# Output projection with seven products: weight sums in half steps, fetches moved, output stage ordered from a list of durations

## The chip, the cores and the metric

The kernel runs on one core of a Trainium2 chip. The metric is the device time of one execution in microseconds (us); lower is better. Five engines take part, each with its own queue of instructions that it works off in order: TensorE (PE, with its weight loads shown apart as PEld), VectorE (DVE), ScalarE (ACT), GpSimd (POOL) and SyncE (SP). SP only starts DMA transfers here; POOL and ScalarE start some too. L12 stands for line 12 of the kernel before.

## The reference

One layer of a hybrid trunk: 1024 latent tokens and 128 context tokens of width 1024 go through a modulated norm, one input projection, a gMLP group and an attention group of 4 heads, and one output projection. The change lies in the softmax loop and in the output projection:

```python
def _back(x, gate, a_out, attn, g_b, w_o):
    y = jnp.concatenate([a_out, attn * jax.nn.silu(g_b)], axis=-1) @ w_o
    return x + gate * y
...
        s = jnp.concatenate(logits, axis=-1).astype(jnp.float32) * ATTN_SCALE
        p = jax.nn.softmax(s, axis=-1).astype(v_all.dtype)
        return jnp.einsum('bhqk,bkhv->bqhv', p, v_all)
...
    y_prompt = _rmsnorm(xp, final_g)
    y_sample = _rmsnorm(xs, final_g)
```

All of it is fp32, and w_o is 1024 x 1024.

## The kernel before

**Tiles.** The tokens are nine tiles of 128: tiles 0 to 7 hold the latent tokens, tile 8 the context. An fp32 matmul is done as three passes of a faster type: each operand is split into a part hi and a remainder lo, and hi x hi, lo x hi and hi x lo are added in PSUM. The split is a cast (ScalarE or POOL, `pool_copy` L115) and a subtraction on VectorE (`lo_of` L112), called the low below.

**Softmax loop** (about 320 to 525 us). Each round takes two heads: their scores on TensorE, maxima on VectorE, exponentials on ScalarE (L1490), and `divide` (L1493 to 1501), which normalises a head's row e on POOL (L1496). Merged with the scores of a round runs the value stream of the round before: transposes of e (pT, L1554), their split (ph L1558 on ScalarE, pl L112 on VectorE), three matmuls each, and the result joined into mixB (L1599).

**Weight sums.** The output projection multiplies pairs of tiles by w_o with seven half-size products instead of eight. They need four sums T1 to T4 of the blocks of w_o (each 512 x 512, in four pieces). A unit `t_unit` (L1860) makes a quarter of one k piece of all four: `t_load` (L1854) brings traw from memory, four subtractions on POOL (L809), two casts on ScalarE (thi, L1876), two lows on VectorE, eight stores to the DRAM buffer tdram (SP). There are eight units; `divide` starts one behind each of the heads 5 to 12. `t_fetch` and `t_piece` (L1891, L1896) bring pieces back through POOL's queue.

**Loads of w_o.** The blocks themselves come through `wo_piece` and `next_load` (L1634 to 1662): SP loads piece k into wor, POOL casts two halves into area, VectorE makes their lows. Pieces 0 to 4 share one raw buffer; a load starts only when the low before it has been read. Pieces 5 to 7 use the slots of e.

**Output stage.** `pair(n)`, n = 0 to 3, takes two tiles and runs its products in the order EARLY, the last pair in FINAL (L1791, L1792). The left operand of a product is a block of the two tiles (A11, A12, A22) or a sum of blocks (S1 to S4, made by four `s_sums` on POOL); it is split into one of the five slots of `ring` (L1812) by `split` (L2067: two copies on ScalarE, one of them to PSUM, and a low on VectorE). A product is 12 matmuls, four k pieces of three passes, into one PSUM bank. What comes after a product (`after`, L2111) adds it to others on VectorE, multiplies by the gate and adds the residual row xr on POOL or VectorE; `norm` and `finish_last` give the final norm and the stores of y. The context tile needs all eight pieces of w_o and is multiplied by `plain` without sums, between the last transposes.

**What sets the order.** Nothing is scheduled at run time: Python code places each instruction. `run` carries a model clock forward and `later(dt, fn)` puts work at a modelled time; `merged` mixes two lists by their modelled lengths. At each softmax round a line asks whether a pool is to be opened. A class `Plan` is there too, used in an earlier stage: it holds steps with an engine, a cost, the steps they depend on, a priority and resources, and places at each modelled moment the step of best priority that can run.

## Time and profile before

| what | us |
|---|---|
| median of 3 runs | 643.28 |
| the runs | 643.28, 644.11, 641.68 |
| the profiled execution | 645.44 |
| its span, first to last instruction | 643.7 |
| PE busy | 605.0 |
| PEld busy (overlaps PE) | 543.6 |
| DVE busy | 435.8 |
| ACT busy | 328.6 |
| POOL busy | 215.4 |

The mean granted TensorE clock of the profiled execution is 0.974. The span is cut into 40 equal slices, each with a digit for the busy tenths of an engine; a row of the timeline gives the start in us, the duration, the engine, the line, the operation and its operands, and in brackets how long the engine was idle just before and which instruction ended that. The rows of transfers at the end of a page give the destination, the source, the queue, the number of transfers, the size of one and the median time from issue to landing.

### The profile page before, as it was taken

To read this page: it belongs to the slowest core of one execution; us is meant where nothing else is said; L and a number is where in the kernel's file an instruction comes from. 1 tells how busy PE (TensorE), PEld (TensorE's weight loads), DVE (VectorE), ACT (ScalarE), POOL (GpSimd) and SP (SyncE) were. 2 spreads that over 40 slices of the span, in tenths; PEclk is the share of its full clock that TensorE was granted. 3 is DMA by queue.
4 is the path that set the end of the run, shared out by engine and by line. 5 is a ranking of instruction groups with operands and counts; after the bars stand their busy time and mean duration, and the time that the engine had idled before them with its cause. 6 is when DMAs were issued, how large, how long until landed. Compare 5 with 4: busy or idle time off the path is not lost. (4 is left out here: it accounts for less than half of the span.)

```text
span 643.7 us, 10209 instructions
## 1 busy us (share of the span) xinstructions
PE 605.0 (94%) x3659; PEld 543.6 (84%) x3659; DVE 435.8 (68%) x931; ACT 328.6 (51%) x758; POOL 215.4 (33%) x262
## 2 busy tenths in 40 slices
PE   8899999999999999999999978899999999799980
PEld 6678899999989999999988867799999988587760
DVE  4793468996655685666787756577767755387885
ACT  6566753345333345555665555555466433365541
POOL 2470111000000002333634755235322346267652
PEclk9999999999999999999999988899999999899995
DMA  8982010003332141000021656400111129933311
GB/s 320 403 329 66 1 34 10 24 1 130 131 133 66 44 162 38 13 1 1 8 66 50 196 168 203 137 1 2 34 34 34 56 78 369 348 112 118 130 67 66
DMA packets 31779, 67.33 MB, mean 105 GB/s; under 512 B 3424, under 2 KB 18672, under 8 KB 31216
## 3 DMA queue, kind: packets, MB, share of 16 engines
q1 hardware_dynamic: 28704, 58.09, 26.0%
q0 software_dynamic: 2880, 8.39, 3.7%
q8 instruction: 29, 0.48, 0.3%
q14 instruction: 22, 0.18, 0.1%
q10 hardware_dynamic: 144, 0.20, 0.1%
HBM read 53.45 MB, written 13.21 MB: 104 GB/s over the span
## 5 line engine op out<-in xcount | busy, mean ns | idle before, releaser
L1496 POOL TENSOR_SCALAR e<-e,rs 128x1280 f32<-128x1280 f32 x32 | 45.1, 1409 | 108.7 <-DVE rs L1495 88.2
L112 DVE TENSOR_TENSOR pl<-pT,ph 128x512 fp32r<-128x512 f32 x81 | 55.2, 685 | 34.0 <-ACT ph L1558 32.9
L1490 ACT ACTIVATE e<-s,nb,scl 128x256 f32<-128x256 f32 x64 | 56.0, 879 | 28.9 <-DVE nb L1484 28.9
L1558 ACT CAST ph<-pT 128x512 fp32r<-128x512 f32 x80 | 45.3, 588 | 40.8 <-PE pT L1554 37.2
L1237 POOL TENSOR_TENSOR kr<-z,rope 128x64 f32<-128x64 f32 x8 | 2.6, 321 | 172.2 <-ACT z L1246 172.2
L1554 PE MATMUL pT<-ident,e 128*128 128x128 f32 x320 | 49.3, 277 | 9.2 <-DVE rs L1494 4.1
L752 PE MATMUL tp<-area,w 128*128 128x384 f32 x288 | 52.4, 338 | 0.0
L752 PEld LDWEIGHTS tp<-area,w 128*128 128x128 f32 x288 | 50.3, 188 | 0.4
L1554 PEld LDWEIGHTS pT<-ident,e 128*128 128x128 f32 x320 | 37.9, 142 | 14.2 <-DVE pl L112 7.5
L1578 PE MATMUL o<-ph,vh 128*128 128x256 f32 x160 | 48.5, 303 | 0.1
L1580 PE MATMUL o<-ph,vl 128*128 128x256 f32 x160 | 46.0, 288 | 0.0
L1579 PE MATMUL o<-pl,vh 128*128 128x256 f32 x160 | 45.8, 286 | 0.0
L1480 DVE TENSOR_REDUCE m<-s 128x1 f32<-128x1024 f32 x32 | 38.9, 1215 | 1.5 <-PE s L1511 1.5
L1507 PE MATMUL s<-kch,area 128*128 128x512 f32 (+2 forms) x100 | 39.7, 397 | 0.0
L1510 PE MATMUL s<-krh,area 128*128 128x512 f32 (+2 forms) x100 | 36.0, 360 | 0.0
L1508 PE MATMUL s<-kcl,area 128*128 128x512 f32 (+2 forms) x100 | 35.9, 359 | 0.0
L1509 PE MATMUL s<-kch,area 128*128 128x512 f32 (+2 forms) x100 | 35.8, 358 | 0.0
L1511 PE MATMUL s<-krl,area 128*128 128x512 f32 (+2 forms) x100 | 35.7, 357 | 0.0
L976 PE MATMUL tp<-area,w 128*128 128x384 f32 x192 | 35.0, 337 | 0.0
L976 PEld LDWEIGHTS tp<-area,w 128*128 128x128 f32 x192 | 33.6, 188 | 0.4 <-issue 0.4
L1578 PEld LDWEIGHTS o<-ph,vh 128*128 128x128 f32 x160 | 31.1, 194 | 1.8 <-ACT os L1588 0.3
L1579 PEld LDWEIGHTS o<-pl,vh 128*128 128x128 f32 x160 | 31.1, 194 | 1.4
(660 smaller groups left out, 1740.5 us busy)
## 6 DMA issues: line engine op xcount, KB each, us to landing
ada<-in_ada_ss SPq DMA_DIRECT2D x16, 512.0 KB, 8.1
w2r<-in_w_t SPq DMA_DIRECT2D x12, 512.0 KB, 4.4
x<-in_x SPq DMA_DIRECT2D x9, 512.0 KB, 7.1
xr<-in_x SPq DMA_DIRECT2D x9, 512.0 KB, 10.8
adag<-in_ada_g SPq DMA_DIRECT2D x4, 1024.0 KB, 4.9
traw<-in_w_o SPq DMA_DIRECT2D x16, 256.0 KB, 3.7
tdram<-thi SPq DMA_DIRECT2D x32, 128.0 KB, 3.4
tdram<-traw SPq DMA_DIRECT2D x32, 128.0 KB, 2.8
```

The lines of the kernel that those rows point to most:

```text
L112: V.tensor_tensor(lo, src, f32(hi), op=ALU.subtract)
L752: T.matmul(tps[i, g][:, :GW], w_[i][:, k, :], x_[k, g], start=k == 0 and j == 0, stop=k == NK - 1 and j == 2)
L976: T.matmul(tps[c, 2][:, :GW], w_[c][:, k, :], x_[k, 2], start=k == 0 and m == 0, stop=k == NK - 1 and m == 2)
L1480: V.tensor_reduce(m[:, 0:1], lat_, axis=AX.X, op=ALU.max)
L1490: S.activation(e[:, sl], src, AF.Exp, bias=nb, scale=scl[:, t : t + 1], accum_out=su[:, i : i + 1])
L1496: G.tensor_scalar(e, e, rs, 0.0, op0=ALU.mult, op1=ALU.add)
L1507: T.matmul(ps, qh_, kch[:, sl], start=True, stop=False)
L1554: T.transpose(ps[:, w : w + P], es[t, h][:, c * P : (c + 1) * P], ident)
L1558: later(0.5, lambda: S.copy(ph[:, :w], ps[:, :w]))
L1578: T.matmul(o, vh[:, kt, :], ph[:, sl], start=c == 0, stop=False)
L1579: T.matmul(o, vh[:, kt, :], pl[:, sl], start=False, stop=False)
L1580: T.matmul(o, vl[:, kt, :], ph[:, sl], start=False, stop=c == n - 1)
```

## The change

**Half steps.** `t_unit` takes a part: the first does two subtractions, the second the other two and what follows them. There are 16 such parts, one behind each of the heads 5 to 18 and two behind head 19. The modelled times of casts and lows are moved.

On POOL, in the softmax loop (e11 to e13 are the rows of three heads in a row, traw the loaded blocks of w_o), before:

```order
L1496 TENSOR_SCALAR e11_3663<-e11_3663,rs11_3662 128x1280
L809 TENSOR_TENSOR traw0_3725<-traw0_3725 128x256 x4
L1496 TENSOR_SCALAR e12_3778<-e12_3778,rs12_3777 128x1280
L809 TENSOR_TENSOR traw1_3728<-traw1_3728 128x256 x4
L1496 TENSOR_SCALAR e13_3855<-e13_3855,rs13_3854 128x1280
L809 TENSOR_TENSOR traw2_3824<-traw2_3824 128x256 x4
```

and in the same place now:

```order
L1496 TENSOR_SCALAR e11_3663<-e11_3663,rs11_3662 128x1280
L809 TENSOR_TENSOR traw0_3725<-traw0_3725 128x256 x2
L1496 TENSOR_SCALAR e12_3775<-e12_3775,rs12_3774 128x1280
L809 TENSOR_TENSOR traw0_3725<-traw0_3725 128x256 x2
L1496 TENSOR_SCALAR e13_3837<-e13_3837,rs13_3836 128x1280
L809 TENSOR_TENSOR traw1_3728<-traw1_3728 128x256 x2
```

Two subtractions stand where four stood, and a unit takes two heads.

**Loads of w_o.** The pool that holds wor can only be opened when the units have given their room back. It is opened three rounds later (21 for 15); pieces 0 and 1, and the first splits and sums of the output stage, are asked for there, pieces 2 to 4 one round later, as before.

On VectorE, around the last head of the loop (pl70_2 to pl70_4 are lows of the value stream, area1 the lows of w_o's pieces made from wor, kcl5 that of piece 5), before:

```order
L112 TENSOR_TENSOR pl70_2_5810<-pT70_2_5804,ph70_2_5809 128x512
L112 TENSOR_TENSOR area1_119<-wor4_5685,area1_119 128x512 x2
L1599 TENSOR_TENSOR mixB_2045<-mixB_2045,at61_5829 128x2x128
L112 TENSOR_TENSOR pl70_3_5846<-pT70_3_5840,ph70_3_5845 128x512
L112 TENSOR_TENSOR kcl5_5753<-wor5_5754,kch5_5752 128x512
L112 TENSOR_TENSOR pl70_4_5869<-pT70_4_5863,ph70_4_5868 128x512
```

and now (line numbers of the changed file, where L1601 is the old L1599):

```order
L112 TENSOR_TENSOR pl70_2_5796<-pT70_2_5790,ph70_2_5795 128x512
L112 TENSOR_TENSOR area1_119<-wor2_5673,area1_119 128x512 x2
L1601 TENSOR_TENSOR mixB_2045<-mixB_2045,at61_5816 128x2x128
L112 TENSOR_TENSOR area1_119<-wor3_5811,area1_119 128x512 x2
L112 TENSOR_TENSOR area1_119<-wor4_5825,area1_119 128x512 x2
L112 TENSOR_TENSOR pl70_3_5849<-pT70_3_5843,ph70_3_5848 128x512
L112 TENSOR_TENSOR pl70_4_5871<-pT70_4_5865,ph70_4_5870 128x512
L112 TENSOR_TENSOR kcl5_5741<-wor5_5827,kch5_5740 128x512
```

Piece 2 stands where piece 4 stood, and the lows of pieces 3 and 4 have come ahead of the next low of the value stream.

**Fetches of the sums.** T2's four transfers are asked for right behind the last head instead of in the run of `plain`, T3's after `plain(4, 1)` instead of `plain(6, 1)`. T1 and T4 become steps of the list; T4's four pieces stand between the four sums of the second pair on POOL, where before all eight stood ahead of them.

**Output stage.** All its steps (products, copies, splits, sums, gates, norms, transfers) go into a `Plan` with a duration and their dependences, and its run places them. Every product takes a bank of the pool psw (five banks) and the PSUM copy of a split one of pst (two); before, S1 and S2 had pst and the copy one bank of pso. In the last pair S3 comes ahead of S4, tile 6's left half (A12) is gated and added on VectorE, tile 7's parts go through POOL, and tile 6 is scaled in halves on ScalarE, which issues their stores. The loads of residual rows wait in the list for the stores of y whose room they take.

On VectorE, in the last pair (S3_3, S4_3, A22_3 are products, xr6 and xr7 the rows of the two tiles, fs16 to fr6 the small steps of tile 6's norm), before:

```order
L806 TENSOR_TENSOR S4_3_6687<-S4_3_6687,mixB_2045 128x512
L2089 TENSOR_TENSOR S4_3_6687<-S4_3_6687,gate0_6056 128x512
L2090 TENSOR_TENSOR xr6_6527<-S4_3_6687,xr6_6527 128x512
L2048 TENSOR_TENSOR fs16_6726<-fss6_6685 128x1
L2050 TENSOR_SCALAR fv6_6727<-fs16_6726 128x1
L2059 RECIPROCAL fr6_6729<-ft6_6728 128x1
L2143 TENSOR_TENSOR mixB_2045<-S3_3_6703,gate0_6056 128x4x128
L2060 TENSOR_TENSOR fw6_6730<-fr6_6729 128x1
L2144 TENSOR_TENSOR xr7_6529<-xr7_6529,mixB_2045 128x512
```

and now:

```order
L2245 TENSOR_TENSOR P7_3_6724<-S3_3_6691,gate0_6104 128x512
L2249 TENSOR_TENSOR S3_3_6691<-S3_3_6691,gate0_6104 128x512
L2250 TENSOR_TENSOR xr7_6559<-S3_3_6691,xr7_6559 128x512
L2248 TENSOR_TENSOR xr7_6559<-P7_3_6724,xr7_6559 128x512
L806 TENSOR_TENSOR S4_3_6711<-S4_3_6711,mixB_2045 128x512
L2236 TENSOR_TENSOR S4_3_6711<-S4_3_6711,gate0_6104 128x512
L2266 TENSOR_TENSOR A22_3_6730<-A22_3_6730,gate0_6104 128x256
L2237 TENSOR_TENSOR xr6_6464<-S4_3_6711,xr6_6464 128x512
```

The four operations on S3 stand ahead of those on S4, and the product by the gate goes to a new bank P7 instead of mixB.

The diff, cut to its core:

```diff
-            if units and units[0] in traw:
-                unit_of[0](units.pop(0))
+            if units and units[0][0] in traw:
+                n_ = 1 + (len(units) == 2)
+                for _ in range(n_):
+                    unit_of[0](*units.pop(0))
...
-        FINAL = (("A11", "B11"), ("A12", "B21"), ("S2", "T2"), ("S1", "T1"), ("S4", "B22"), ("S3", "T3"), ("A22", "T4"))
+        FINAL = (("A11", "B11"), ("A12", "B21"), ("S2", "T2"), ("S1", "T1"), ("S3", "T3"), ("S4", "B22"), ("A22", "T4"))
...
-        def t_unit(u):
+        def t_unit(u, part):
 
             k, c = divmod(u, 2)
             raw = traw[u]
             b11, b12, b21, b22 = (raw[:, i, :] for i in range(4))
-            sub(G, b11, b12, b11)
-            sub(G, b12, b22, b12)
+            if part == 0:
+                sub(G, b11, b12, b11)
+                sub(G, b12, b22, b12)
+                return
             sub(G, b22, b22, b11)
             sub(G, b21, b21, b22)
...
-                later(3.2 + 1.5 * i, lambda i=i: high(i))
-                later(4.0 + 1.5 * i, lambda i=i: low(i))
+                later(3.2 + 1.8 * i, lambda i=i: high(i))
+                later(4.6 + 1.8 * i, lambda i=i: low(i))
...
-            need(("blk", q))
+                need(("blk", q))
...
+                units += [(u, part) for u in range(8) for part in range(2)]
                 unit_of.append(t_unit)
-            if 2 * c + LEAD + 1 == 15:
+            if 2 * c + LEAD + 1 == 21:
...
             if k == 4 and i == 1:
                 for n in range(4):
-                    t_piece(2, n, flat[2][2 + n])
-            if k == 6 and i == 1:
-                for n in range(4):
                     t_fetch(3, n, woh[n][:, 512:1024], wol[n][:, 512:1024])
...
         later(6.0, lambda: (wo_need(4), early_split(2)))
+        later(2.0, lambda: [t_piece(2, n, flat[2][2 + n]) for n in range(4)])
...
+    plan = Plan()
+    plan.free.update(T=0.0, V=0.5, S=0.5, G=0.0, D=0.0)
+    plan.resources.update(w=1, raw=2)
...
+    def fetch(key, fn, deps=()):
+        last_ = [fetched[0]] if fetched[0] else []
+        step(key, "D", 1.35, fn, [*deps, *last_], 0, lag=1.8)
+        fetched[0] = "|" + key
...
-    for n, (m, k) in enumerate([(1, k) for k in range(4)] + [(4, k) for k in range(4)]):
-        t_piece(m, k, tpiece[n])
-        if n == 3:
-            load_gate(0, tag="gate0")
-    load_gate(1, tag="xr", bufs=4)
-    load_xr(8)
-    load_xr(0)
-    load_xr(1)
-    fg = ep.tile([P, 1024], F32, tag="fg", name="fg")
...
+    for m, n in ((1, 0), (4, 4)):
+        for k in range(4):
+            fetch(f"T{m}{k}", lambda m=m, k=k, n=n: t_piece(m, k, tpiece[n + k]))
+        if m == 1:
+            fetch("gate0", lambda: load_gate(0, tag="gate0"))
+    fetch("gate1", lambda: load_gate(1, tag="xr", bufs=4))
+    for t in (8, 0, 1):
+        fetch(f"x{t}", lambda t=t: load_xr(t))
+    fetch("fg", lambda: nc.sync.dma_start(fg, I["final_g"].broadcast_to([P, 1024])))
...
+        def scale_half(c):
+            S.activation(xr[t][:, c], xr[t][:, c], AF.Copy, scale=cell["fr"])
+            nc.scalar.dma_start(O["y"][t][:, c], xr[t][:, c])
+
+        if by_half:
+            for h_, c in (("L", L), ("R", R)):
+                on_s(f"y{t}{h_}", lambda c=c: scale_half(c), [*prev, f"fg{t}{h_}"], 1.5)
             return
...
+    for q in range(3, len(queue)):
...
+        ready = {"S1": "s0", "S2": "s1", "S3": "s2", "S4": "s3"}.get(name)
+        deps = [f"{ready}{n}"] if ready and n else []
+        room = {3: ["pl7"], 4: ["pl7"], 5: []}.get(q) if q < 6 else [name_of(q - 5)]
...
-            cell["raw"] = pso.tile([P, 512], F32, tag="o", name=f"raw{q}").rearrange("p (k c) -> p k c", k=4)
...
+            cell["raw"] = pst.tile([P, 512], F32, tag="t", name=f"raw{q}").rearrange("p (k c) -> p k c", k=4)
...
+        on_s(f"hi{q}", lambda q=q, n=n, name=name: S.copy(ring(q)[:, 0], block(n, name)), [*deps, *room], 1 + 0.01 * q)
+        on_s(f"raw{q}", raw, [*deps, f"hi{q}"], 1 + 0.01 * q, takes=("raw",))
+        on_v(f"lo{q}", lambda q=q, cell=cell: lo_of(ring(q)[:, 1], cell["raw"], ring(q)[:, 0]), [f"raw{q}"], 1 + 0.01 * q, gives=("raw",))
...
+    def on_t(key, cost, fn, deps, **kw):
+        step(key, "T", cost, fn, [*deps, *([turn[0]] if turn[0] else [])], 1, lag=0.25, **kw)
+        turn[0] = "|" + key
...
-            else:
-                kind = (pst, "t") if name in ("S1", "S2") else (psw, "w")
-                banks[name] = kind[0].tile([P, 512], F32, tag=kind[1], name=f"{name}_{n}")
...
+            def whole(q=q, name=name):
+                bank(name)
                 product(q, banks[name])
...
+            on_t(P_(name), 2.73, whole, deps, takes=("w",))
...
+        on_s(D_("k"), lambda: S.copy(K, ps("A11")), [P_("A11"), *s_done, f"hi{at_['A11']}", f"raw{at_['A11']}"], 2, gives=("w",))
+        on_v(D_("c11"), lambda: add(V, ps("A12"), ps("A12"), K), [P_("A12"), D_("k")], 2)
         if last:
-            banks["A22"] = psw.tile([P, 512], F32, tag="w", name=f"A22_{n}")
-            finish_last(b, 7 * n + 6, banks["A22"])
-
-    def x_row(t, old):
-        if ("y", old) in made:
-            load_xr(t)
+            on_v(D_("m11"), lambda: V.tensor_tensor(banks["A12"], banks["A12"], gate[0][:, L], op=ALU.mult), [D_("c11")], 2)
+            on_v(D_("a11"), lambda: V.tensor_tensor(xr[a][:, L], banks["A12"], xr[a][:, L], op=ALU.add), [D_("m11"), f"x{a}"], 2)
+            square(a, 0, lambda: banks["A12"], L, [D_("a11")])
+            step(f"free{n}", "N", 0.0, lambda: None, [f"sq{a}.0"], 0, gives=("w",))
...
+            for t in PAIRS[nx]:
+                old = [f"y{PAIRS[n - 1][t % 2]}"] if n else (["g80", "g81"], ["y8"])[t % 2]
+                fetch(f"x{t}", lambda t=t: load_xr(t), old)
...
+        on_g(D_("m21"), lambda: G.tensor_tensor(X, K, gL(), op=ALU.mult), [D_("u2"), f"hi{at_['S1']}", f"raw{at_['S1']}"], 2)
+        on_g(D_("a21"), lambda: add(G, half(b, L), half(b, L), X), [D_("m21"), f"x{b}"], 2.1)
+        on_g(D_("m22"), lambda: G.tensor_tensor(C, W, gR(), op=ALU.mult), [D_("u4"), f"hi{at_['S2']}", f"raw{at_['S2']}"], 2.2)
+        on_g(D_("a22"), lambda: add(G, half(b, R), half(b, R), C), [D_("m22"), f"x{b}"], 2.3)
+        on_g("fg6L", lambda: G.tensor_tensor(xr[a][:, L], xr[a][:, L], fg[:, L], op=ALU.mult), [f"sq{a}.0", "fg"], 2.5)
+        on_v(D_("c12"), lambda: add(V, ps("S4"), ps("S4"), W), [P_("S4"), D_("u4")], 2)
+        on_v(D_("m12"), lambda: V.tensor_tensor(banks["S4"], banks["S4"], gate[0][:, R], op=ALU.mult), [D_("c12")], 2)
+        on_v(D_("a12"), lambda: V.tensor_tensor(xr[a][:, R], banks["S4"], xr[a][:, R], op=ALU.add), [D_("m12"), f"x{a}"], 2)
+        square(a, 1, lambda: banks["S4"], R, [D_("a12")], 2)
+        on_g("fg6R", lambda: G.tensor_tensor(xr[a][:, R], xr[a][:, R], fg[:, R], op=ALU.mult), [f"sq{a}.1", "fg"], 3)
+        norm(a, 0.6, True)
...
+            on_v("z0", z0, [P_("S3")], 1, takes=("w",))
+            on_v("z1", lambda: V.tensor_tensor(xr[b][:, R], banks["P7"], xr[b][:, R], op=ALU.add), ["z0", D_("a22")], 1)
+            on_v("z2", lambda: V.tensor_tensor(banks["S3"], banks["S3"], gate[0][:, L], op=ALU.mult), ["z0"], 1.1)
+            on_v("z3", lambda: V.tensor_tensor(xr[b][:, L], banks["S3"], xr[b][:, L], op=ALU.add), ["z2", D_("a21")], 1.1)
...
+    plan.run()
```

More of the change, by code (lines that the diff above doesn't have):

```diff
@@ new lines, in finish_plain @@
+    def finish_plain():
+        for j, c in enumerate((L, R)):
+            ps = wps[8][j]
+            on_v(f"g8{j}", lambda ps=ps, c=c: V.tensor_tensor(ps, ps, gate[1][:, c], op=ALU.mult), ["pl7", "gate1"], 3.0)
+            on_v(f"a8{j}", lambda ps=ps, c=c: V.tensor_tensor(xr[8][:, c], ps, xr[8][:, c], op=ALU.add), [f"g8{j}", "x8"], 3.0)
+            square(8, j, lambda ps=ps: ps, c, [f"a8{j}"])
+        step("free8", "N", 0.0, lambda: None, ["sq8.0", "sq8.1"], 0, gives=("w", "w"))
+        norm(8, 3.5)
@@ L2100, in pair @@
         half = lambda t, c: view(xr[t][:, c])
-        gL, gR = view(gate[0][:, L]), view(gate[0][:, R])
+        gL, gR = (lambda: view(gate[0][:, L])), (lambda: view(gate[0][:, R]))
         banks = {}
-        def gated_add(src, g, t, c, dt, j=None):
-            later(dt, lambda: G.tensor_tensor(src, src, g, op=ALU.mult))
-            plus(src, t, c, dt + 1.3, j)
-        def plus(src, t, c, dt, j=None):
-            later(dt, lambda: G.tensor_tensor(half(t, c), half(t, c), src, op=ALU.add))
-            if j is not None:
-                later(dt + 1.5, lambda: square_of(t, j, src, c.start, c.stop))
@@ L2154, in step_of, with bank @@
-        def step_of(i):
-            q = 7 * n + i
+        q0 = 7 * n
+        at_ = {queue[q0 + i][1]: q0 + i for i in range(7)}
+        P_ = lambda name: f"p{n}{name}"
+        D_ = lambda s: f"{s}.{n}"
+        ps = lambda name: view(banks[name])
+        def bank(name):
+            banks[name] = psw.tile([P, 512], F32, tag="w", name=f"{name}_{n}")
+        for i in range(6 if last else 7):
+            q = q0 + i
             name = queue[q][1]
+            m = queue[q][2]
+            deps = [f"lo{q}", *([f"{m}{k}" for k in range(4)] if m[0] == "T" else [])]
@@ L2162, in step_of @@
                         plain(7, h_)
+                    plan.made["pl7"] = 2.4
                     product(q, banks[name], ks=[3])
[L2164 to L2170 removed]
@@ L2237, in tile_hymba_step, with last_room @@
+        finish()
+    tail = {}
+    def last_room():
+        tail["z"] = ep.tile([P, 1024], F32, tag="xr", name="zl", bufs=4)
+    finish_plain()
+    for n in range(4):
         pair(n)
-    zl = ep.tile([P, 1024], F32, tag="xr", name="zl", bufs=4)
-    pair(3)
+    step("zl", "N", 0.0, last_room, ["y4", "y5", "x6", "x7"], 0)
+    catch_up(1e9)
+    plan.run()
     final.close()
```

253 lines of the change are left out of this document (123 added, 130 removed).

## The prediction, made before the changed kernel was timed

> **What bounds the kernel now.** I read the page's slices first, then, in the timeline, the starts of one POOL line, then the waits, then single rows around each hole.
>
> ```profile
> PE   8899999999999999999999978899999999799980
> PEclk9999999999999999999999988899999999899995
> ```
>
> A slice is 16.1 us. TensorE is full except in three places: slices 23 to 26 (the softmax loop while the weight sums run), slice 35 (start of the output stage) and the last two. The kernel is TensorE-bound, so a change pays only where it closes one of these holes, and costs where it opens one.
>
> The first hole, measured by the normalisation of each head on POOL. All four rows are of second heads of a round, four rounds apart:
>
> ```profile
> 360.66 1.33 POOL L1496 TENSOR_SCALAR e<-e,rs 128x1280 f32<-128x1280 f32 x1 [2.87 <-DVE rs L1495]
> 421.43 1.34 POOL L1496 TENSOR_SCALAR e<-e,rs 128x1280 f32<-128x1280 f32 x1 [6.05 <-DVE rs L1495]
> 457.96 1.34 POOL L1496 TENSOR_SCALAR e<-e,rs 128x1280 f32<-128x1280 f32 x1 [4.97 <-DVE rs L1495]
> 506.16 1.34 POOL L1496 TENSOR_SCALAR e<-e,rs 128x1280 f32<-128x1280 f32 x1 [5.49 <-DVE rs L1495]
> ```
>
> Four rounds take 60.77 us with weight sums and 48.20 us without: **12.6 us** lost, slow clock included. Why, from the waits of 340 to 420 us (total, times, longest) and single rows:
>
> ```profile
> ACT thi L1876 <- POOL traw L809: 13.6, 7, 3.8
> POOL traw L809 <- DMA traw<-in_w_o: 2.8, 4, 1.4
> 382.05 1.12 PE L1554 MATMUL pT<-ident,e 128*128 128x128 f32 x4 [2.02 <-DVE mixB L1599]
> 361.96 3.69 POOL L809 TENSOR_TENSOR traw<-traw 128x256 f32<-128x256 f32 x4
> 466.32 0.69 DVE L112 TENSOR_TENSOR area<-wor,area 128x512 fp32r<-128x512 f32 x1
> 466.50 0.56 ACT L1490 ACTIVATE e<-s,nb,scl 128x256 f32<-128x256 f32 x1 [1.45 <-DVE nb L1484]
> ```
>
> Each unit is four subtractions (3.69 us) behind one head, and its cast stands in ScalarE's queue before they are done: ScalarE waits up to 3.8 us, and the exponentials and casts of ph behind it wait too. Two units a round also bring the loads of traw too late.
>
> **The change part by part.**
>
> *Half steps.* The same 32 subtractions, 16 casts, 16 lows and 80 transfers now take 15 heads instead of 8, so one unit a round. Two subtractions (1.85 us, half of 3.69) follow a head; the first cast of a unit reads what the head before made, so it finds its data. In a quiet round there is room: ScalarE idles 1.45 us ahead of the 466.50 row, where a cast fits, and VectorE already carries one such low at 466.32. A unit's transfers get 12 us instead of 6 to 8, so the traw waits go. Only the last unit still does four subtractions at once. I take **-12.0**. Bounds: all 12.6 plus half a microsecond of the round before, -13.1; and, if in each of seven rounds half of one half step (0.9 of 1.85) still delays the normalisation behind it, -6.3.
>
> *Loads of w_o moved behind them.* The pool for the raw loads opens three rounds later (21 for 15), and pieces 0 to 4 share one buffer. Piece 2 therefore stands where piece 4 stood, directly behind the last head, and pieces 3 and 4 come after it, one after the other. The rows that time this:
>
> ```profile
> 517.13 1.33 POOL L1496 TENSOR_SCALAR e<-e,rs 128x1280 f32<-128x1280 f32 x1 [5.01 <-ACT ph L1558]
> 518.44 1.21 POOL L115 TENSOR_SCALAR area<-wor 128x512 fp32r<-128x512 f32 x2
> 519.78 2.00 DVE L112 TENSOR_TENSOR area<-wor,area 128x512 fp32r<-128x512 f32 x2
> 523.55 0.69 DVE L112 TENSOR_TENSOR pl<-pT,ph 128x512 fp32r<-128x512 f32 x1 [1.44 <-ACT ph L1558]
> 527.33 0.60 PE L1554 MATMUL pT<-ident,e 128*128 128x128 f32 x4
> wor<-in_w_o SPq DMA_DIRECT2D x8, 512.0 KB, 3.8
> xr<-in_x SPq DMA_DIRECT2D x9, 512.0 KB, 10.8
> 529.36 2.33 POOL L1898 DMA_DIRECT2D area<-tdram  x4
> area<-tdram POOLq DMA_DIRECT2D x4, 512.0 KB, 5.5
> ```
>
> VectorE's queue is in order, and the lows of pieces 3 and 4 now stand ahead of the low of pT70_3 (the 523.55 row). Working it out on the clock of before: piece 2's lows end at 521.8 and free the buffer; load 3 takes 3.8 alone, but the four T2 fetches are now issued on POOL just before it, so I take 5.0 (between 3.8 and the 10.8 of loads in a full queue, near the lower, since T2 is 2 MB, some 5 us); casts and lows behind a landing take 0.62 + 0.62 + 0.69 and handovers, 2.1; load 4 is issued at 528.9, lands at 532.7, is split at 534.8; then the low of pT70_3, 0.69: 535.5. TensorE's transpose at 527.33 needs the PSUM bank which that low frees (two banks), so it starts 8.2 to 8.5 us late. Behind it in TensorE's queue is everything. Nothing hides this: the products ahead of 527.33 need pieces 0 to 3 only and are in order. Bounds: 3.8 for load 3, stall 7; 10.8 for load 3, 14.
>
> A stall of that kind also costs clock, which the row of the next stage times (0.63 us a matmul where 0.39 is usual): about **+2.0**. Sum **+10.5**, from +8.5 to +16. The Trainium skill (TensorE: Matmul & The Clock Gate, Part 1: The HAM clock gate) says that about 3.4 us of idling halves the array's clock and that about 3.4 us of work restores it; by that the term would be 1.7 instead of 2.0, an estimate from that page, and the trace shows the drop after waits as short as the 2.02 above.
>
> *The fetches of T2, T3, T1, T4.* T2 goes 10 us earlier, and T4's four pieces are put between the sums of the next pair on POOL.
>
> ```profile
> 545.12 0.39 PE L1902 MATMUL S<-area,ringC 128*128 128x512 f32 x1
> 547.84 0.39 PE L1902 MATMUL S<-area,area 128*128 128x512 f32 x1
> 560.23 0.79 PE L1902 MATMUL A<-vht,ringB 128*128 128x512 f32 x1 [2.70 <-DMA vht<-tdram]
> 562.71 0.80 PE L1902 MATMUL A<-vlt,ringB 128*128 128x512 f32 x1 [0.84 <-DMA vlt<-tdram]
> 564.16 0.63 PE L1902 MATMUL A<-area,ringC 128*128 128x512 f32 x1
> 566.29 0.41 PE L1904 MATMUL A<-area,ringC 128*128 128x512 f32 x1
> 539.97 2.70 POOL L1898 DMA_DIRECT2D tp<-tdram  x5 [0.66 <-DMA area<-tdram]
> vlt<-tdram POOLq DMA_DIRECT2D x1, 512.0 KB, 17.4
> ```
>
> A product is 547.84 - 545.12 = 2.72 us. Seven products in, the one of A11 should start at 545.12 + 5 x 2.72 = 558.7; it starts at 564.16, and its nine matmuls up to 566.29 are 2.1 us instead of 0.23 each: **7.4 us** lost, clock included. T4 is late (17.4 us) behind 9 MB from T3 on. With T2 gone before, T1 and the residual rows are through when T4 is asked for. But its last piece is issued behind four sums (1.27 us each) of which the last waits for a slot of the ring that the fourth product leaves: 545.12 + 2 x 2.72 = 550.6, two copies at about 0.6 on ScalarE, the sum 1.27 and 0.54 to issue (2.70 by five) make 553.6, plus 5.5 to land 559.1; the product wants it three quarters through, at 556.0 + 2.0 = 558.0. And all products share five banks now, two of them held by tile 8, so the product of S1 waits for the VectorE add that frees one, about 1 us. Left over: 1.9. I take **-5.5**, from -6.9 to -2.
>
> *Splits of the ring first.* The list puts the raw copies in two PSUM banks instead of one and the splits ahead of the norms; the small stalls in pairs 1 and 2 go.
>
> ```profile
> 582.83 0.50 PE L1904 MATMUL A<-tp,area 128*128 128x512 f32 x1 [0.66 <-DVE area L112]
> 622.84 0.39 PE L1904 MATMUL A<-tp,ringC 128*128 128x256 f32 x1 [0.90 <-DVE ringC L112]
> 625.46 0.28 PE L1904 MATMUL A<-vlt,ringC 128*128 128x256 f32 x1
> 622.26 1.28 POOL L2110 TENSOR_TENSOR xr<-xr,mixB 128x512 f32<-128x512 f32 x1 [5.72 <-DVE mixB L2120]
> 629.48 0.69 DVE L2143 TENSOR_TENSOR mixB<-S,gate 128x512 f32<-128x512 f32 x1 [0.83 <-POOL xr L2110]
> 635.83 0.42 DVE L2200 TENSOR_TENSOR A<-A,gate 128x256 f32<-128x256 f32 x1
> 639.68 0.37 ACTq L2230 DMA_DIRECT2D out_y<-zl  x1
> ```
>
> Two pairs at 0.66: **-1.3**, bounds -2 and +2 (the new order may delay another split by as much).
>
> *The end.* TensorE ends at 625.7, the span at 643.7. In between VectorE waits for POOL, whose first add of the last pair comes only at 622.26, so that 629.48 starts four VectorE operations late and 635.83, the last half's multiply, runs 10 us after its matmuls. The new order gives tile 6's left half to VectorE, so POOL's four operations of tile 7 (1.28 each) can start when the S2 product is added (622.84 - 0.90 - 3 x 2.72 = 613.8, and 0.69: 614.5) and end by 621; product S3 comes before S4, so its four VectorE operations (0.69) and three of S4 fill 619.2 (one product after S1's end at 616.5) to 624.8 while TensorE still works. TensorE ends 0.9 earlier (the 622.84 wait), at 624.8; then 0.5 of backlog; the chain from 635.83 to 639.68, 3.85; seven small VectorE operations of tile 6 put into it, 1.2; two scalings of tile 6 with their DMA issues on ScalarE ahead of the last one, 1.2 beyond what VectorE does meanwhile; and 3.65 (639.68 to the end of the span, less its 0.37 of issue) + 0.4. That is 635.6, **-7.9** after rounding down for POOL and VectorE running together. Bounds -9 and -4.
>
> **Sum.** -12.0 + 10.5 - 5.5 - 1.3 - 7.9 = -16.2. The profiled execution took 645.44 us (span 643.7), so 629.2; the median of the three runs shown, 643.28, is 2.2 lower, so **627 us**.
>
> **Rivals.** *The loads are hidden after all:* pieces 3 and 4 cost nothing, because something not visible in the order covers them; -26.7 instead of -16.2, 616.6 us. For it speaks only that 3.8 us is short; against it, that two loads, two splits and the buffer make one chain in front of an in-order queue. *The half steps give little:* POOL's sums behind every head delay the next normalisation; attention gives 6.3, or the loads cost 16 because T2 fills the queues: 633 us, and 638 if both. For it POOL's two half steps in every round, which quiet rounds lack; against it ScalarE's 1.45 us gap. *Slower:* the five shared banks. If the wait for a bank that I see once at S1 came at each of the 26 products, 1.1 us each, the output stage would grow by 28.6 and the total be 656; it decides from 0.6 us a product, where 15.6 eats the whole gain. For it: VectorE is in order and frees four of the seven banks. Against: after the first pair tile 8's two banks are back, and a bank has two more products, 5.4 us, to come free.
>
> **Chances.** The forecast, with its stall near 10: 0.60. Hidden loads: 0.10. Little from the half steps or dearer loads: 0.14. Banks: 0.16, most of it large enough to be slower. Runs of this kernel spread over 0.4%, so 0.5% (3.2 us) is what can be told from no change: faster below 640.1, slower above 646.5. The forecast, the hidden loads and 0.08 of the 0.14 end below 640.1: faster 0.78; the rest of the 0.14 and 0.03 of the banks lie within: same 0.09; slower 0.13. The likeliest case alone spans 620 to 635; with half of the first and the lighter part of the others, 616 to 641, which leaves out 0.05 below and 0.13 above.
>
> **What would show it.** Right: normalisations of second heads 12.0 to 12.3 us apart from the third round on; ScalarE's wait of thi for traw under 4 us in total; one hole of 7 to 12 us on TensorE about 10 us after the last head's normalisation, ahead of a pT transpose, with VectorE waiting there for a load or a cast of wor; load 4 issued some 7 us after load 3; vht and vlt wait under 2 us; the span ends about 11 us after the last matmul. Wrong: no hole there (then 617), or holes at the first matmul of many products with VectorE as releaser (then the banks), or T4 waits of more than 5 us.

## The result, and the profile after

The changed kernel takes 642.78 us (median of 12 runs), the kernel before 643.14 (12 runs); the ratio is 0.999, with a 95% interval of 0.9977 to 1.0004. That cannot be told from no change, where 627 us and a range of 616 to 641 had been forecast. The profiled execution has a span of 640.9 us, 2.8 less than that of before. The slices of its page, TensorE and its granted clock:

```profile
PE   7999999999999999999999999999999949989990
PEclk8999999999999999999999999999999978999996
```

The first hole of before (slices 24 to 26) is gone, one at slice 33 is new, the small one of slice 35 is now in slice 36, and the last slice is as empty as it was. TensorE's instructions stand in the same order in both kernels up to the last pair, so each can be held against itself. What the change makes of its start times, point by point:

| point | before | after | after less before |
|---|---|---|---|
| first normalisation on POOL | 322.04 | 323.22 | +1.2 |
| last normalisation on POOL | 517.13 | 507.98 | -9.2 |
| a matmul of o behind the new hole | 530.56 | 534.36 | +3.8 |
| a matmul of the first product with T1 | 551.24 | 556.15 | +4.9 |
| a matmul behind T4's first product | 568.63 | 570.10 | +1.5 |
| end of the last matmul | 625.74 | 624.13 | -1.6 |
| end of the span | 643.7 | 640.9 | -2.8 |

The differences between the rows are the terms of the prediction, each by itself: the loop -10.3, the loads of w_o +13.0, the fetches +1.1 and -3.4 (-2.3 in all), the splits of the ring -3.1, the end -1.2. (The +1.2 of the first row is no part of the change: the programs are alike up to there, and that point lies between 321.48 and 323.83 in the executions below.)

**The loop**, in the timeline of the changed kernel, by the same four heads as before:

```profile
360.40 1.62 POOL L1496 TENSOR_SCALAR e<-e,rs 128x1280 f32<-128x1280 f32 x1 [4.53 <-ACT ph L1560]
410.01 1.62 POOL L1496 TENSOR_SCALAR e<-e,rs 128x1280 f32<-128x1280 f32 x1 [3.91 <-ACT ph L1560]
448.68 1.34 POOL L1496 TENSOR_SCALAR e<-e,rs 128x1280 f32<-128x1280 f32 x1 [6.39 <-DVE rs L1495]
497.00 1.34 POOL L1496 TENSOR_SCALAR e<-e,rs 128x1280 f32<-128x1280 f32 x1 [5.47 <-DVE rs L1495]
```

Four rounds with half steps take 49.6 us (60.8 before), the four quiet ones 48.3. In the view of waits from 340 to 450 us the cast of thi no longer waits for POOL's subtractions at all, where it had waited 13.6 us.

**The new hole**, in the timeline (lines of the changed file: L1556 the transposes, L1935 to L1937 the context tile's products, L1650 the loads of w_o, L1902 the fetches):

```profile
510.44 2.33 POOL L1902 DMA_DIRECT2D area<-tdram  x4
511.99 0.33 SPq L1650 DMA_DIRECT2D wor<-in_w_o  x1
519.64 1.20 POOL L115 TENSOR_SCALAR area<-wor 128x512 fp32r<-128x512 f32 x2 [6.87 <-DMA wor<-in_w_o]
520.30 0.80 PE L1935 MATMUL w<-area,area 128*128 128x512 f32 x1 [2.67 <-POOL area L115]
525.39 1.20 POOL L115 TENSOR_SCALAR area<-wor 128x512 fp32r<-128x512 f32 x2 [4.56 <-DMA wor<-in_w_o]
526.04 2.10 DVE L112 TENSOR_TENSOR area<-wor,area 128x512 fp32r<-128x512 f32 x2 [4.07 <-POOL area L115]
528.80 1.11 PE L1556 MATMUL pT<-ident,e 128*128 128x128 f32 x4 [6.15 <-DVE pl L112]
```

T2's 2 MB are asked for on POOL just ahead of piece 3, which then takes 7.6 us to land (511.99 to 519.64, a load alone 3.8). Piece 4 follows in the same buffer; its lows stand on VectorE ahead of the low that frees the transposes' bank. TensorE stands 2.67 us for the cast of piece 3 and 6.15 us for that low, and its matmuls behind each wait last 0.63 us where 0.39 is usual.

**T4**, in the timeline and the rows of transfers:

```profile
555.38 0.47 PE L1906 MATMUL S<-tp,ringA 128*128 128x512 f32 x1 [0.83 <-ACT area L2119]
556.91 0.57 POOL L1902 DMA_DIRECT2D vlt<-tdram  x1
565.89 0.50 PE L1906 MATMUL A<-vlt,ringB 128*128 128x512 f32 x1 [2.57 <-DMA vlt<-tdram]
```

```profile
vlt<-tdram POOLq DMA_DIRECT2D x1, 512.0 KB, 8.9
```

One wait of 2.57 us is left of the two of before, and the product with T1 waits 0.83 us. That row names ScalarE, whose cast was long done; what ends at that time (555.28) is VectorE's add of the S2 product, which frees a bank.

**The end**, VectorE and POOL in the last pair:

```profile
617.02 0.69 DVE L806 TENSOR_TENSOR A<-A,mixA 128x512 f32<-128x512 f32 x1
618.88 0.68 DVE L806 TENSOR_TENSOR mixA<-S,mixA 128x512 f32<-128x512 f32 x1
619.71 1.29 POOL L2230 TENSOR_TENSOR mixA<-mixA,gate 128x512 f32<-128x512 f32 x1 [4.80 <-DVE mixA L806]
620.14 0.15 DVE L2083 RECIPROCAL fr<-ft 128x1 f32<-128x1 f32 x1
621.00 1.29 POOL L2234 TENSOR_TENSOR xr<-xr,fg 128x512 f32<-128x512 f32 x1
621.05 1.24 DVE L2085 SCALAR_TENSOR_TENSOR fw<-fw,fv 128x1 f32<-128x1 f32 x1
622.24 1.29 POOL L806 TENSOR_TENSOR xr<-xr,mixA 128x512 f32<-128x512 f32 x1
622.33 1.21 DVE L2086 SCALAR_TENSOR_TENSOR fr<-fw,fr 128x1 f32<-128x1 f32 x1
623.47 0.68 DVE L806 TENSOR_TENSOR mixB<-S,mixA 128x512 f32<-128x512 f32 x1
631.15 0.43 DVE L2266 TENSOR_TENSOR A<-A,gate 128x256 f32<-128x256 f32 x1
```

The add of the S2 product (618.88) comes 5.8 us after that product's last matmul (624.13 less 2.88 for A22 and three products of 2.72: 613.1), and the add of S1 is held up another 2 us by two operations on one number a row that last 1.24 and 1.21 us. They begin with POOL's operations at 621.00 and 622.24 and end with them. The multiply of the last half by the gate (631.15) comes 7.0 us after the last matmul's end (624.13). Held against the list's own modelled times, with the last matmul as the common point, VectorE is on time until the first norm, loses 6.8 us in the norms of tiles 8 and 0 to 2, and is still 5.4 us late at the add of the S2 product.

### The profile page after: what moved, and what is told of

Same layout as the page of the kernel before. It is cut to its first block, busy times and chain, and to the rows that moved or that the text cites. A ratio compares the mean times of both kernels' runs of the same rounds, so it can differ in the third digit from the quotient of the medians.

```text
span 640.9 us, 10218 instructions
## 1 busy us (share of the span) xinstructions
PE 603.0 (94%) x3659; PEld 542.1 (85%) x3659; DVE 444.5 (69%) x931; ACT 329.0 (51%) x760; POOL 218.9 (34%) x263
## 5 line engine op out<-in xcount | busy, mean ns | idle before, releaser
L1556 PE MATMUL pT<-ident,e 128*128 128x128 f32 x320 | 49.1, 276 | 9.5 <-DVE pl L112 9.3
L1556 PEld LDWEIGHTS pT<-ident,e 128*128 128x128 f32 x320 | 37.5, 142 | 15.6 <-DVE pl L112 8.4
L1509 PE MATMUL s<-kch,area 128*128 128x512 f32 (+2 forms) x100 | 39.0, 390 | 0.0
L1511 PE MATMUL s<-kch,area 128*128 128x512 f32 (+2 forms) x100 | 35.2, 352 | 0.0
```

Source lines behind the costliest of these rows:

```text
L1509: T.matmul(ps, qh_, kch[:, sl], start=True, stop=False)
L1556: T.transpose(ps[:, w : w + P], es[t, h][:, c * P : (c + 1) * P], ident)
```

## The experiments

Each time is a median, with its ratio to the kernel before on the same chip and the 95% interval; the changed kernel has 642.8 and 0.999. "The loop" is the time from the first to the last normalisation on POOL.

**1. Pieces of w_o first.** The splits of pieces 0 to 4 go ahead of the other split jobs, so the one buffer comes free a head after each load.

```diff
-        his.append(high)
+        his.append(high) if first is None else his.insert(first, high)
...
-                split_job(lambda c_=c_: pool_copy(hi[:, c_], r[:, c_]), lambda c_=c_: low(c_), ("w", k, i))
+                split_job(lambda c_=c_: pool_copy(hi[:, c_], r[:, c_]), lambda c_=c_: low(c_), ("w", k, i), i if k < 5 else None)
```

> The changed kernel, but the splits of pieces 0 to 4 of w_o go to the front of the list of split jobs, so that a piece gives its raw buffer back one head after its load and all five are split by the last head. Theory (the ledger of TensorE's times): the changed kernel loses 13.0 us between the last head and the first products because pieces 3 and 4 are loaded there; with them loaded before, that goes, and nothing else moves: 12 to 13 us less than the changed kernel, about 630 us; no hole on TensorE before the transpose that started at 528.80; less the up to 0.9 us a round that the extra casts in the rounds may cost. Rival (the hole has another cause: the transposed bank waits for VectorE's backlog, or the queue is full with the T2 pieces): the hole stays, within 2 us of the changed kernel.

629.06 us, ratio 0.978 (0.9752 to 0.9809). The stretch of the hole in the view by windows, changed kernel first, then this one (busy time and count of PE, PEld, DVE, ACT, POOL, then the granted clock):

```profile
508.00:534.00 26.00, 16.64 (x79) 13.07 (x79) 10.76 (x15) 3.62 (x8) 14.51 (x24) 0.74 0.63 212
```

```profile
508.00:534.00 26.00, 25.79 (x164) 22.44 (x163) 13.38 (x22) 8.35 (x18) 15.23 (x26) 1.00 0.75 226
```

79 matmuls at 0.74 of the clock against 164 at 1.00. The loop took 184.98 us instead of 184.76, so the casts in the rounds cost next to nothing. The hole is the loads.

**2. Whole units, pool at 15.** Both halves of a unit behind one head, and the pool of w_o where it was.

```diff
-                n_ = 1 + (len(units) == 2)
-                for _ in range(n_):
+                for _ in range(2):
...
-            if 2 * c + LEAD + 1 == 21:
+            if 2 * c + LEAD + 1 == 15:
```

> The changed kernel, but with both halves of a weight-sum unit behind one head (heads 5 to 12, four subtractions each) and the pool of the raw w_o pieces opened at 15 again, as before the change; everything else as changed. Theory: the half steps give 10.3 us and the later loads take 13.0, so without both the kernel is 2.6 us faster than the changed one, about 640 us. Rival (the half steps alone are what pays, the late loads are mostly hidden by waits that come anyway): 8 us slower than the changed kernel, 651 us.

636.33 us, 0.9886 (0.9861 to 0.991): faster than the changed kernel, by 6.4 and not 2.6. The loop took 190.86 us where the kernel before had 195.09 in its profiled execution; experiment 7 shows how far that number can be trusted. Half steps with late loads are worse than neither.

**3. T2 behind the loads.**

```diff
-        later(6.0, lambda: (wo_need(4), early_split(2)))
-        later(2.0, lambda: [t_piece(2, n, flat[2][2 + n]) for n in range(4)])
+        later(6.0, lambda: (wo_need(4), [t_piece(2, n, flat[2][2 + n]) for n in range(4)], early_split(2)))
```

> The changed kernel, but T2's four transfers are issued behind the casts of piece 4 instead of ahead of those of piece 3. Theory: the load of piece 3 took 7.6 us to landing (511.99 to 519.6) because T2's 2 MB stand in the same transfer engines; without them 3.6, so the hole is 3.5 to 4 us shorter; T2 is not needed for another 15 us. About 639 us. Rival (the load waits for its buffer and the cast, not for the transfer engines): no change, 642.8 us.

638.62 us, 0.9921 (0.9899 to 0.9943). Piece 3 landed by 515.10, 3.3 us after its issue:

```profile
511.83 7.39 SPq L1650 DMA_DIRECT2D wor<-in_w_o  x5
515.10 1.20 POOL L115 TENSOR_SCALAR area<-wor 128x512 fp32r<-128x512 f32 x2 [4.77 <-DMA wor<-in_w_o]
524.36 1.11 PE L1556 MATMUL pT<-ident,e 128*128 128x128 f32 x4 [6.17 <-DVE pl L112]
```

So 4.2 us of the hole came from T2's new place, the rest from the order of the loads.

**4. One tensor operand.** The norm's steps on one number a row, rewritten so that the second value is a per-row scalar.

```diff
-            lambda: V.tensor_tensor(cell["fw"], cell["fr"], cell["fr"], op=ALU.mult),
-            lambda: V.scalar_tensor_tensor(cell["fw"], cell["fw"], -0.5, cell["fv"], op0=ALU.mult, op1=ALU.mult),
-            lambda: V.scalar_tensor_tensor(cell["fr"], cell["fw"], 1.5, cell["fr"], op0=ALU.add, op1=ALU.mult),
+            lambda: V.tensor_scalar(cell["fw"], cell["fr"], cell["fr"], None, op0=ALU.mult),
+            lambda: V.tensor_scalar(cell["fw"], cell["fw"], -0.5, cell["fv"], op0=ALU.mult, op1=ALU.mult),
+            lambda: V.tensor_scalar(cell["fr"], cell["fw"], 1.5, cell["fr"], op0=ALU.add, op1=ALU.mult),
```

(and the first sum, and three such steps of the last tile, in the same way)

> The changed kernel, but the small steps of the final norm (128x1) that read two tensors are written as operations with one tensor and a per-row scalar: the same values, the same place and number of instructions. Theory: those with two tensor operands wait for a POOL operation that is running (0.15 us alone, up to 1.29 beside POOL), which puts VectorE 5 to 7 us behind TensorE in the output stage and so makes the end late; with one tensor operand they take 0.15 to 0.2 us each, VectorE is 3 to 5 us less behind, and the span ends 2.5 to 5 us earlier: about 639 us. Rival (VectorE is behind because of the order of the list, not of the durations): under 1 us.

636.46 us, 0.9896 (0.9873 to 0.9919). The groups by line, changed kernel first, then this one (busy us and mean ns of one behind the bar):

```profile
L2085 DVE SCALAR_TENSOR_TENSOR fw<-fw,fv 128x1 f32<-128x1 f32 x8 | 5.6, 704 | 0.1
L2086 DVE SCALAR_TENSOR_TENSOR fr<-fw,fr 128x1 f32<-128x1 f32 x8 | 4.8, 599 | 0.2
L2084 DVE TENSOR_TENSOR fw<-fr 128x1 f32<-128x1 f32 x8 | 3.6, 450 | 0.1
L2083 DVE RECIPROCAL fr<-ft 128x1 f32<-128x1 f32 x8 | 1.2, 154 | 2.1 <-ACT ft L2079 2.1
```

```profile
L2086 DVE TENSOR_SCALAR fr<-fw,fr 128x1 f32<-128x1 f32 x8 | 1.7, 211 | 0.2
L2085 DVE TENSOR_SCALAR fw<-fw,fv 128x1 f32<-128x1 f32 x8 | 1.7, 210 | 0.1
L2084 DVE TENSOR_SCALAR fw<-fr 128x1 f32<-128x1 f32 x8 | 1.7, 210 | 0.1
```

The span ends 11.1 us after the last matmul (16.8 in the changed kernel, 18.0 before). The reciprocal, with one operand, had 0.15 us all along. VectorE in the last pair, by the add of the S2 product and the last half's multiply:

```profile
613.11 0.68 DVE L806 TENSOR_TENSOR mixA<-S,mixA 128x512 f32<-128x512 f32 x1
624.71 0.43 DVE L2266 TENSOR_TENSOR A<-A,gate 128x256 f32<-128x256 f32 x1
```

The last matmul ends at 623.07 here. So the add comes 1.1 us after its product (5.8 in the changed kernel), and the multiply 1.6 us after the last matmul (7.0). What is left has a like cause: the scaling of a whole row in the norm (L2092, 128x1024, two tensors) was not rewritten, and its seven instances take 1.30 to 2.43 us, where the list has 1.25.

**5. The kernel before with one operand.** The same edit of the same lines there.

> The kernel before, with the norm's small steps written with one tensor operand, nothing else. The small steps with two operands took 13.2 us in all in its output stage and 17.3 us in the changed one, against 6.8 us in that form. Theory: the kernel before loses less to them and its end is set by POOL's late first add of the last pair, so the gain is smaller than the changed kernel's 6.3: 1.5 to 3.5 us, about 641 us. Rival (the same 6 us, so the new order has no part in the end): 637 us.

642.3 us, 0.9986 (0.9961 to 1.001): no difference that can be told, and 17.2 us from the last matmul to the end. So the new order has its part in the end: only with it are these steps in the way.

**6. Old times.** Half steps, with the casts and lows at the modelled times of before.

```diff
-                later(3.2 + 1.8 * i, lambda i=i: high(i))
-                later(4.6 + 1.8 * i, lambda i=i: low(i))
+                later(3.2 + 1.5 * i, lambda i=i: high(i))
+                later(4.0 + 1.5 * i, lambda i=i: low(i))
```

> The changed kernel, but the casts and lows of a unit's second half step are placed at the old modelled times (casts 3.2 and 4.7, lows 4.0 and 5.5). Whole units with the new times took 190.86 us from the first to the last normalisation, the kernel before 195.09, the changed one 184.76. Theory A: the half steps alone suffice, since the data are there when the cast comes: within 1 us of the changed kernel. Theory B (the later places are worth 4.2 us in either case): loop 189, total 647 us.

641.42 us, 0.9964 (0.9938 to 0.9989); the loop took 182.86 us, 1.9 less than with the new times (182.86 to 183.11 in the four executions with half steps and the old times, here and in experiments 10 to 12). A round with half steps takes 12.1 us instead of 12.4. Theory A, and beyond it: the later places cost a little.

**7. Whole units, old times.** Edits 2 and 6 together; its loop is that of the kernel before.

> The changed kernel with whole units behind heads 5 to 12, the pool at 15, and the old modelled times: up to the last head the program is that of the kernel before. Its loop took 195.09 us in one execution of that kernel and 192.45 in another kernel with the same loop; with the new times 190.86. Theory A (the times matter for whole units): loop 192.5 to 195, total 638 to 641 us. Theory B (the loop with whole units simply varies, because it waits for loads): 190 to 192, total within 1.5 us of the 636.3 with the new times.

638.02 us, 0.9903 (0.9878 to 0.9929), loop 192.06. That program's loop took 195.09, 192.45 (in experiment 5) and 192.06, so it varies by 3 us from one execution to the next, where six executions with half steps and the new times lie between 184.75 and 184.99. The result lies between the two theories: the times are worth 1.2 us by these two executions, which is less than the spread. Nearly all of the spread lies in the four rounds from which the prediction read its loss: they took 60.77, 58.04 and 57.65 us in the three executions, and the four quiet rounds 48.20 or 48.21 in each.

**8. T4 first.** All eight transfers of T1 and T4 ahead of the sums on POOL, on the changed kernel.

```diff
-            fetch(f"T{m}{k}", lambda m=m, k=k, n=n: t_piece(m, k, tpiece[n + k]))
+            fetch(f"T{m}{k}", lambda m=m, k=k, n=n: t_piece(m, k, tpiece[n + k]), cost=0.6)
...
+    fetch("pad", lambda: None, cost=6.0)
     fetch("gate1", lambda: load_gate(1, tag="xr", bufs=4))
```

> The changed kernel, but T4's four transfers are issued straight behind T1's, ahead of the four sums of the second pair on POOL; the loads of the second gate and of the rows keep their later place. Theory: TensorE waited 2.57 us for vlt because it was issued at 556.91, behind three sums, and took 8.9 us to land; issued some 8 us earlier it is there, the sums come 2.2 us later, which the ring covers: 2.3 to 2.6 us less than the changed kernel, 640.3 us. Rival (the transfers are slow because the queue is full, and issuing them together only makes each slower; and the late sums hold up the splits): no gain, 642.8 or 1 us more.

641.66 us, 0.9966 (0.9941 to 0.9992), not to be told from the changed kernel. The wait for vlt went, and the wait at the first product with T1 grew from 0.83 to 2.29 us; VectorE had stood 4.82 us for the gate's load.

**9. Three edits at once: 1, 4 and 8.**

> The changed kernel with three edits together: the splits of w_o's pieces ahead of the other split jobs, the norm's small steps with one tensor operand, and T4's four transfers issued ahead of the sums of the second pair. Theory (three holes in three places of one chain of TensorE's times, so they add): 13.7 + 6.3 + about 2.4 less than the changed kernel, 620.5 us. Rival (once TensorE is earlier, VectorE's and POOL's backlog of the output stage is what sets the end): 624 to 626 us.

626.01 us, 0.973 (0.9694 to 0.9766), 3 us better than the first alone where 8.7 was expected. VectorE and TensorE in the timeline:

```profile
542.80 0.69 DVE L2199 TENSOR_TENSOR mixB<-f,gate 128x512 f32<-128x512 f32 x1 [6.26 <-DMA gate<-gdram]
543.75 0.77 PE L1906 MATMUL S<-tp,ringA 128*128 128x512 f32 x1 [3.70 <-DVE mixB L2199]
```

The gate's load, asked for at 530.77 in the midst of the 4 MB of T1 and T4 (527.39 to 532.18), kept VectorE 6.26 us, and TensorE waited for the bank that this operation frees.

**10. Edits 1, 4 and 6.**

> The changed kernel with the splits of w_o's pieces put first, the norm's small steps with one tensor operand, and the old modelled times of casts and lows; T1 and T4 fetched as changed. Theory: 629.1 (pieces first alone) less 6.3 (one operand) less 1.9 (the loop with the old times, 182.86 against 184.76 us) = 621 us, TensorE's end near 609.5, the span 11 us longer. Rival (VectorE's backlog decides the end wherever TensorE ends): 624 us or more.

622.08 us, 0.9662 (0.9638 to 0.9687), 11.6 us from the last matmul to the end: the three gains add (621 expected).

**11. Edits 1, 4, 6 and 8, and 2.5 MB of other loads put later**, into ScalarE's queue behind the third product.

```diff
+    last_ = ["p0S2"]
+    for key, fn in (("gate1", gate_late), *((f"x{t}", lambda t=t: load_late(t)) for t in (8, 0, 1)), ("fg", lambda: nc.scalar.dma_start(fg, I["final_g"].broadcast_to([P, 1024])))):
+        step(key, "S", 0.4, fn, list(last_), 0.5, lag=4.0)
+        last_ = ["|" + key]
```

> The three edits, and T4's transfers straight behind T1's with the loads that are not needed then (the second gate, rows 8, 0, 1, and the final gain) moved to ScalarE's queue behind the third product of the first pair. Theory: with T4 first alone the first gate landed 12 us after its issue and VectorE stood 6.3 us for it, which turned T4's wait into one for a PSUM bank; with 2.5 MB less in the queue the gate and T4 both come in time: 2.5 to 3.5 us less than three edits, 618 us. Rival (4 MB of T1 and T4 alone make the gate late): no gain, TensorE waits at the first product of T1 for VectorE.

623.78 us, 0.9688 (0.9662 to 0.9715), no gain; VectorE stood 6.82 us for the gate and TensorE 4.25 at that product. The rival holds: the other loads were not what made the gate late. Without T4's early transfers (experiment 10) there is no such wait.

**12. T4 together behind the first sum.** Edits 1, 4 and 6, and T4's four transfers where POOL stands idle.

```diff
+            fetch(f"T{m}{k}", lambda m=m, k=k, n=n: t_piece(m, k, tpiece[n + k]), ["|s01"] if m == 4 else (), 0.6 if m == 4 else 1.35)
...
+            on_g(f"s1{nx}", fns[1], [f"s0{nx}", *(["|T43"] if nx == 1 else [])], 1)
```

> The three edits, and T4's four transfers together behind the first sum of the second pair instead of one behind each sum; POOL stood idle 3.3 us there, and the first gate has been asked for by then. Theory: the gate lands as in the three edits, vlt some 5 us earlier, so TensorE's wait of 2.7 us for vlt goes and no wait of more than 1 us comes at the first product of T1: 619.5 us. Rival (any earlier T4 shares the transfer engines with the gate, so that the wait only moves): 621 to 624 us.

619.63 us, 0.9623 (0.9596 to 0.965): the best version, 3.8% below the kernel before. Its page and the row of vlt:

```profile
PE   8899999999999999999999999999999999999992
PEclk9999999999999999999999999999999999999997
```

```profile
547.14 0.50 PE L1906 MATMUL A<-vlt,ringB 128*128 128x512 f32 x1 [0.21 <-DMA vlt<-tdram]
```

## Why the prediction was wrong, step by step

The largest miss is the end. By the prediction's own terms, profiled execution against profiled execution:

| term | predicted | measured |
|---|---|---|
| half steps | -12.0 | -10.3 |
| loads of w_o | +10.5 | +13.0 |
| fetches of T | -5.5 | -2.3 |
| splits of the ring (0.9 of it was counted with the end) | -2.2 | -3.1 |
| from the last matmul to the end | -7.0 | -1.2 |
| ahead of the loop | 0 | +1.2 |
| sum | -16.2 | -2.8 |

(Each row is rounded by itself.) By the medians the sum is -0.4: the profiled execution of before was 2.3 us above its kernel's median.

**Half steps: the mechanism right, the size from a single execution.** The cast finds its data, and ScalarE's wait is gone. But the 12.6 us of the forecast were read from one execution. In the other two executions of the same loop (experiments 5 and 7) the same four rounds lose 9.8 and 9.4 us, and the half steps give 7.7 and 7.3 us against them, where the table has 10.3. The prediction then took 2.2 us off once more for the median, although this execution was slow in this very loop; why it was, no run shows. The changed times of casts and lows, which the prediction counted at nothing, cost 1.9 us.

**Loads: the mechanism right, the size 2.5 short.** The hole stands where it was put, with the chain that was named; "I take 5.0" for load 3 was the wrong number: it took 7.6 with T2's 2 MB in front of it. Experiment 3 took that away and gained 4.2 us, experiment 1 took the whole hole away and gained 13.7. The hole is in two parts: 2.67 us of it is a wait of the context tile's products for piece 3, which the prediction held to be "in order".

**Fetches: right on the issue, wrong on the landing.** Less was to be had than the prediction read from the trace of before: the matmuls from 564.16 to 566.29 are six and not nine, and the seventh product starts at 567.94 where it would have started at 561.4 without the waits (545.12 + 6 x 2.72), so 6.5 us were lost there and not 7.4. The last piece of T4 was asked for about when the prediction had it (556.9; 553.6 on the clock of before and 3.8 for the delay by then is 557.4). "5.5 to land" was 8.9. The bank that holds up S1 cost 1.1, as said. The five shared banks did nothing more: no other product waits for one, so that rival fell.

**Splits of the ring: right.** The waits of pairs 1 to 3 are gone; the end of the matmuls gained 3.1 us by that, where the idle times in the rows of before make 2.2.

**The rivals.** Hidden loads: no, the hole is there. Little from the half steps: partly, 7.3 to 10.3 where that case had 6.3. Dearer loads: partly, 13.0 where that case had up to 16.

**The end: the step that failed.** The sentence was that POOL's four operations of tile 7 "can start when the S2 product is added (622.84 - 0.90 - 3 x 2.72 = 613.8, and 0.69: 614.5)". It takes for granted that VectorE is free when TensorE is done, and the sum has "0.5 of backlog" for it. VectorE was 5.4 us behind, POOL began at 619.71, and where the prediction had 0.5 us from the last matmul to the last half's multiply it was 7.0. What put VectorE behind is mostly the small steps of the norms: without their waits it is 1.6 us. The prediction has them once, as "seven small VectorE operations of tile 6" at 1.2 us, and not at all for the seven tiles before (8 and 0 to 5); beside POOL a single one takes up to 1.29. With one operand the end comes 11.1 us after the last matmul; the prediction had 10.8. So the order does what was worked out for it, once VectorE keeps up, and experiment 5 shows that the edit without the order gives nothing that can be told. The bound of -4 was too near because it did not come from any row of this wait, although the trace of before has such rows: the same step of the norm took 0.15 to 1.22 us there.

The page of the Trainium skill that bears on it (SBUF: State Buffer, section SBUF: two separate sides) says that VectorE and GpSimd share one pair of ports as an exclusive lock, which a VectorE operation with two SBUF inputs contends for with a GpSimd operation that reads SBUF, and that the one that comes second waits for the whole of the other. The trace agrees: 1.24 and 1.21 us with two inputs beside POOL, 0.15 with one. It also goes the other way: POOL's multiply by the gate at 624.22 took 2.24 us instead of 1.29 while VectorE ran a scaling of 1.27 us with two inputs.

The misses of the loads, the fetches and the end have one thing in common. Each number was taken from rows in which the resource was less loaded: a load of 3.8 alone, a landing of 5.5, a step of 0.15. The change put more work next to each.

## What to carry to other kernels

When an order made from a list of durations runs late, hold each step's planned time against the trace: the first step that lasts longer than its entry is the one to mend, and here it was the cheapest entry of all. A single buffer whose release waits in a common first-in-first-out list is a chain of loads; give its users the front of the list before moving anything else. A transfer that is moved earlier is to be priced with what stands in the queue at its new place, and so are the transfers that it now stands in front of. A loss read from one execution is to be held against another of the same code before it enters a sum.

## What was not expected of the hardware

An operation on 128 single numbers, 0.15 us by itself, costs as much as a POOL operation on 128x512 (1.3 us) when both start together, and only if it reads two tensors; a second value given as a per-row scalar costs nothing of the kind (0.20 to 0.22 us in all 32 instances of the four kinds of step). In the output stage the four kinds of small steps with two operands and the reciprocal made 18.5 us of VectorE's time, against 8.0 after the edit. And the loop with whole units varied by 3 us between executions of the same instructions, more than ten times what the loop with half steps did. Its waits differ (POOL waits for a load of traw up to 1.4 us in the slowest of the three and 0.8 in the others, ScalarE's casts for POOL 13.6, 11.6 and 9.3 us in all), but what makes them differ is not shown.
